# A hybrid sparse-attention and RWKV-7 block: the triangular inverse's levels split into two halves of the heads, and new delays in the order's table

## The chip, the cores and the metric

The kernel runs on 1 core of one Trainium2 chip. Times are device microseconds (us) of one execution. Before the change the median of 3 runs is 951.49 us (948.81 to 954.71).

## The reference, cut to what matters

One decoder block on x of 1 x 512 x 1024 in float32. After an RMS norm, one combined projection makes the columns of two branches that run side by side, and of two gates:

```
q, k = rms_norm(q), rms_norm(k)            # 8 heads of 64
scores = sum_h w_h * relu(q_idx_h . k_idx)  # the indexer, 8 heads of 64
sel = top_k(causal scores, 128)             # for each query
y_attn = softmax(q . k[sel] + rel_bias) @ v[sel]

for t in range(512):                        # RWKV-7, per head
    s_a = state @ (-kk_t)
    state = state * d_t + s_a b_t^T + v_t k_t^T
    y_t = state @ r_t
y_rwkv = (group_norm(y) + bonus * v) * g    # bonus = sum(r * k * r_k)

h = x + (sigmoid(g1) * (y_attn @ w_a) + sigmoid(g2) * (y_rwkv @ w_r)) @ w_out
out = h + (silu(n @ w_gate) * (n @ w_up)) @ w_down    # n = rms_norm(h), width 2816
```

## The kernel before, in words

**Weights and dense products.** All weights come in one stream of 129 chunks of 128x1024 floats. SP fetches a chunk, ACT rounds it to a high part, `w_hi` (L239), and POOL or, for every third chunk from number 17 on, DVE subtracts that from the raw chunk to make the low part, `w_lo` (L243). A dense product is three passes on PE for each 128 rows of the contraction: high by high, high by low, low by high (`dense_t`, L255 to L264), each a matmul of 512 columns. The activations' two parts are named `xnh` and `xnl`.

**The attention.** `queries` and `keys` (L471 to L515) take two heads at a time: ACT squares the projection from PSUM (L475, L493) and copies it; some time later `rest` sums the squares over a head on PE (`head_sums`, the "key sums"), POOL takes the power -0.5 (L500), ACT broadcasts it (L501), and, 6.5 units later, PE flips it, DVE multiplies, and ACT and DVE copy the parts of the keys (`split_heads`, L456 to L463, tiles `kh`, `kl`). DVE meanwhile runs the selection of the 128 keys, with rounds of MAX8 and MATCH_REPLACE. `attention` (L519) goes through 32 units, 4 blocks of 128 queries by 8 heads: one step makes the logits of a unit (tile `lg`, whose exponential is ACT's, L574), the flips of the unit two before (L169), and the product with the values `vt` of the one three before.

**The recurrence.** It is computed in 4 blocks of 128 tokens, each two chunks of 64. `operands` (L692) makes the scaled keys of a pair of heads, and its `rest` the bonus products from POOL's `ag` (L709). `matrices` (L740) makes the chunks' triangular matrices (`kr`, `kb`), and `invert` (L777 to L836) their inverses by doubling: five levels, in each of which PE multiplies `l16` (printed as `l` or `l_144`) by `tt` for 8 heads of 64 columns, DVE masks that into `rr` (L806), PE multiplies again twice, ACT copies one product to `tt` (L811) and DVE the other to `uu` (L814). All of these are f16 matmuls in PSUM tiles of tag "i", of which there are two banks. With 4 blocks that makes 20 levels. `steps` (L845) carries the state; `head_norm` (L917) normalises a block's output and multiplies by the gate of `zg` (`g2a`, `g2b`) on PE, in whose course POOL broadcasts the bonus to `bv` (L947) and DVE writes `zv`. The product `yr` (L1045 to L1049) needs the last head norm; it follows the second group of gates (`gr`, "gate matmuls").

**The order.** `Streams` (L98 to L122) writes the program's order before anything runs. Each part is a generator with a rank; it yields a delay, or the name of a signal to wait for. A clock, `st.now`, moves forward by a model time with each matmul, and of the parts whose time has come the one of lowest rank goes on. The dense products have rank 9, so they fill what the others leave. The delays stand in the table `L` (L89 to L91): `sums` before the key and query sums, `attn` between two steps of the attention for each block of queries, `bonus` before a bonus product, `inv_*` in the inverse. PE's instructions keep this order; on ACT, DVE and POOL the order follows from it.

Of the kernel before, what the change touches and what calls it, by code (L numbers as in the profile page):

```python
# [13 lines left out]
AF = mybir.ActivationFunctionType  # L14
# [4 lines left out]
H, N = 8, 64  # L19
# [63 lines left out]
for _n, _c in _PARS:  # L83
# [2 lines left out]

L = dict(norm=3.0, normed=1.3, score=0.4, pick=0.15, rms=6.5, sums=2.5, attn=(1.0, 0.6, 0.4, 0.35), attn_out=2.0, sig=0.3,  # L89
         prep=5.0, oper=6.0, bonus=6.0, mat=0.5, mats=2.8, inv_u=3.25, inv_t=1.4, inv_r=1.4, inv_n=0.9, inv_e=1.8,  # L90
         inv=1.8, vals=0.6, st_b=1.0, st_u=1.36, st_m=1.4, hn_b=4.55, hn_n=6.55, hn_g=2.0)  # L91
POOL_ONLY = 17
COPIES = 23
# [34 lines left out]
def hybrid_block(ctx: ExitStack, tc: tile.TileContext, x, first, rows, consts, lora, rel_bias, stream, out):  # L128
    nc = tc.nc
# [125 lines left out]
    def dense_t(ps, wt, c, act, t0=0, t1=S):  # L255

        k = len(act)
        for j in range(k):
            xh, xl = act[j][0][:, t0:t1], act[j][1][:, t0:t1]
            hi, lo = wt[j][0][:, c], wt[j][1][:, c]  # L260
            mm(ps, hi, xh, start=(j == 0), stop=False)
            mm(ps, hi, xl, start=False, stop=False)
            mm(ps, lo, xh, start=False, stop=(j == k - 1))
            yield 0.0  # L264

# [206 lines left out]
    def queries(j, ps):  # L472
# [15 lines left out]

        st.add(3, rest(), L["sums"])

# [285 lines left out]
    def invert(t):  # L776

        l16 = l16s[t % 2]
        U, T = blocks("uu", 1), blocks("tt", 1)
        nc.vector.tensor_mul(U, l16, lev1[:, None, :].to_broadcast([128, H, 128]))  # L780
        yield L["inv_u"]
        for g in range(2):
            ps = bank("i").rearrange("q (h t) -> q h t", h=4)
            for j in range(4):
                mm(ps[:, j], U[:, 4 * g + j], eye16, start=True, stop=True)
            nc.scalar.activation(T[:, 4 * g:4 * g + 4], ps, AF.Copy)
        for e in range(2):
            br = BLK[e]
            for g in range(2):
                hs = slice(g, H, 2)  # L790
                nc.gpsimd.tensor_sub(l16b[br, hs, br], A[t, e][g][br, :, br], l16[br, hs, br])
        yield L["inv_t"]
        for i in range(1, 6):
            s = 2 ** i
            two = lambda q, w: q.rearrange("q h (g w s) -> q h g w s", w=2, s=s)[:, :, :, w]
            one = lambda q, h, w: q[:, h].rearrange("q (g w s) -> q g w s", w=2, s=s)[:, :, w]
            four = lambda q: q.rearrange("q (h g s) -> q h g s", h=H, s=s)
            o = CONST_AT["level"][0] + (i - 1) * 64
            mask = con[:, o:o + 64].rearrange("q (g s) -> q g s", s=s)[:, None].to_broadcast([128, H, 64 // s, s])
            R = blocks("rr", 2)  # L800
            nc.gpsimd.tensor_copy(two(R, 1), eye16.rearrange("q (g w s) -> q g w s", w=2, s=s)[:, None, :, 1]  # L801
                                  .to_broadcast([128, H, 64 // s, s]))
            ps = bank("i")
            for h in range(H):
                mm(ps[:, h * 64:h * 64 + 64], l16[:, h], one(T, h, 0), start=True, stop=True)
            nc.vector.tensor_mul(two(R, 0), four(ps), mask)  # L806
            yield L["inv_r"]
            p1, p2 = bank("i"), bank("i")
            for h in range(H):
                mm(p1[:, h * 64:h * 64 + 64], U[:, h], one(R, h, 0), start=True, stop=True)  # L810
            nc.scalar.activation(two(T, 0), four(p1), AF.Copy)  # L811
            for h in range(H):
                mm(p2[:, h * 64:h * 64 + 64], R[:, h], one(U, h, 1), start=True, stop=True)
            nc.vector.tensor_copy(two(U, 1), four(p2))  # L814
            yield L["inv_n"]
        E = blocks("ee", 2, "rr")
        for g in range(2):
            ps = bank("i").rearrange("q (h t) -> q h t", h=4)
            for j in range(4):
                h = 4 * g + j  # L820
                mm(ps[:, j], l16b[:, h], T[:, h], start=True, stop=False)
                mm(ps[:, j], l16[:, h], T[:, h], start=False, stop=True)
            nc.vector.scalar_tensor_tensor(E[:, 4 * g:4 * g + 4], ps, -1024.0,
                                           eye1k[:, None, :].to_broadcast([128, 4, 128]), op0=OP.mult, op1=OP.add)
        yield L["inv_e"]
        U32 = unit("u32")
        for g in range(2):
            ps = bank("i").rearrange("q (h t) -> q h t", h=4)
            for j in range(4):
                mm(ps[:, j], E[:, 4 * g + j], U[:, 4 * g + j], start=True, stop=True)  # L830
            for q in BLK:
                hs = slice(4 * g, 4 * g + 4)
                nc.vector.scalar_tensor_tensor(hv(U32)[q, hs], ps[q, :, q], 1.0 / 1024.0, U[q, hs, q],
                                               op0=OP.mult, op1=OP.add)
        U32s[t] = U32
        st.signal(f"inv{t}", L["inv"])  # L836
# [374 lines left out]
```

## Time and profile before

| what | value |
|---|---|
| median of 3 runs | 951.49 us (948.81 to 954.71) |
| the profiled execution's own time | 951.66 us |
| its span in the trace | 949.9 us |
| PE busy (matmuls) | 911.4 us, 96% |
| DVE, ACT, POOL busy | 406.5, 344.5, 365.4 us |
| mean granted clock of PE | 0.99 |

The span runs from the first to the last instruction of the trace. Engines work side by side, so their busy times overlap; PE is TensorE's matmuls, DVE VectorE, ACT ScalarE, POOL GpSimd, SP the engine that issues most transfers. The stages by time, as the tiles in the trace show them: up to 50 us the norm and the first projections, to 107 us queries and keys with the selection, to 225 us the attention beside the projections of the recurrence, to 300 us the preparation of the recurrence, to 500 us its inverses and steps beside the gates, to 600 us the branch products and the output projection, and to the end the FFN.

### The profile page before, as it was taken

The page shows a single profiled execution, that of the slowest core. Times are in us where ns is not written, and L with a number is a line of the kernel's source. Part 1 is how long each engine was busy: PE and PEld are TensorE (multiplying, and loading weights), DVE is VectorE, ACT ScalarE, POOL GpSimd, SP SyncE. Part 2 cuts the span into 40 slices and gives each one's busy share as a digit, 9 for nine tenths or more (in the row PEclk, how much of TensorE's full clock was granted, in tenths as well). Part 3 has the DMA queues.
Part 4 walks back from the last instruction along what each step waited for, and adds up shares of the span by engine and source line. Part 5 has one row for each costly group of instructions (what it writes and reads, how often), then busy time and mean ns, then how long its engine had stood idle before and what let it go on. Part 6 is the DMA issues. An engine that isn't in the chain of part 4 may idle for free.

```text
span 949.9 us, 13573 instructions
## 1 busy us (share of the span) xinstructions
PE 911.4 (96%) x5526; PEld 765.4 (81%) x5526; DVE 406.5 (43%) x796; ACT 344.5 (36%) x548; POOL 365.4 (38%) x242
## 2 busy tenths in 40 slices
PE   7999899899989999999998999999999999999998
PEld 5988797688767777878886998888888888888886
DVE  4389898873573546573534616111111111100111
ACT  5554565543542433233423324323223232221120
POOL 6425532203264353525415632443534344432321
PEclk9999899999999999999999999999999999999999
DMA  6321232101222120201142332233232332332431
GB/s 230 92 79 44 88 117 68 45 1 59 86 67 67 46 67 23 68 20 50 46 133 79 94 94 68 89 94 106 88 111 89 99 101 90 91 108 89 138 107 44
DMA packets 24173, 77.77 MB, mean 82 GB/s; under 512 B 2869, under 2 KB 4366, under 8 KB 24112
## 3 DMA queue, kind: packets, MB, share of 16 engines
q1 hardware_dynamic: 20688, 72.49, 24.3%
q10 hardware_dynamic: 3424, 4.43, 1.7%
q8 instruction: 43, 0.70, 0.3%
q14 instruction: 18, 0.15, 0.0%
HBM read 74.53 MB, written 2.38 MB: 81 GB/s over the span
## 4 chain that ended last, share of the span: by engine, by line
PE 79%; DVE 11%; ACT 3%; POOL 3%; issue 3%; DMA 1%; SPq 0%; ACTq 0%; POOLq 0%; DVEq 0%
PE ps_d L162 57%; PE ps_c L162 11%; PE ps_i L162 9%; DVE score L437 2%; DVE max L436 2%; PE ps_c L169 2%; DVE score L424 1%; POOL w_lo L243 1%; DMA xa<-in_x_dram 1%; DVE qs L460 1%; PE ps_i L169 1%; ACT w_hi L239 1%; ACT lg L574 0%; POOL bb L700 0%; DVE w_lo L243 0%
## 5 line engine op out<-in xcount | busy, mean ns | idle before, releaser
L243 POOL TENSOR_TENSOR w_lo<-w_raw,w_hi 128x1024 fp32r<-128x1024 f32 (+1 forms) x94 | 221.1, 2354 | 366.8 <-ACT w_hi L239 360.0
L239 ACT ACTIVATE w_hi<-w_raw 128x1024 fp32r<-128x1024 f32 x129 | 136.6, 1060 | 370.9 <-PE ps_d L162 213.1
L162 PE MATMUL ps_d<-xnh,w_hi 128*128 128x512 f32 (+2 forms) x360 | 149.7, 416 | 0.0
L162 PE MATMUL ps_d<-hnl,w_hi 128*128 128x512 f32 (+1 forms) x368 | 139.9, 380 | 0.4 <-DVE hnl L336 0.4
L162 PE MATMUL ps_d<-hnh,w_hi 128*128 128x512 f32 (+1 forms) x368 | 139.9, 380 | 0.0
L162 PE MATMUL ps_d<-hnh,w_lo 128*128 128x512 f32 (+1 forms) x368 | 139.7, 380 | 0.0
L162 PE MATMUL ps_d<-xnh,w_lo 128*128 128x512 f32 (+2 forms) x360 | 137.6, 382 | 0.0
L162 PE MATMUL ps_d<-xnl,w_hi 128*128 128x512 f32 (+2 forms) x360 | 137.4, 382 | 0.0
L243 DVE TENSOR_TENSOR w_lo<-w_raw,w_hi 128x1024 fp32r<-128x1024 f32 x37 | 45.6, 1233 | 130.8 <-ACT w_hi L239 130.0
L1095 DVE TENSOR_TENSOR gsig<-ps_d,gsig 128x512 f32<-128x512 f32 x22 | 15.2, 692 | 157.6 <-PE ps_d L162 156.9
L162 PEld LDWEIGHTS ps_d<-hnl,w_hi 128*128 128x128 f32 x368 | 69.2, 188 | 13.8 <-DVE hnl L336 0.6
L162 PEld LDWEIGHTS ps_d<-hnh,w_lo 128*128 128x128 f32 x368 | 69.2, 188 | 13.1
L162 PEld LDWEIGHTS ps_d<-hnh,w_hi 128*128 128x128 f32 x368 | 69.2, 188 | 13.0
L162 PEld LDWEIGHTS ps_d<-xnh,w_lo 128*128 128x128 f32 x360 | 68.9, 191 | 13.1
L162 PEld LDWEIGHTS ps_d<-xnh,w_hi 128*128 128x128 f32 x360 | 69.4, 193 | 11.7 <-issue 2.6
L162 PEld LDWEIGHTS ps_d<-xnl,w_hi 128*128 128x128 f32 x360 | 69.4, 193 | 9.9 <-issue 1.9
L1099 POOL TENSOR_TENSOR ul<-gsig,uh 128x512 fp32r<-128x512 f32 x22 | 31.6, 1434 | 25.3 <-ACT uh L1098 25.3
L801 POOL COPY rr<-eye 128x512 f16<-128x512 f16 x20 | 13.5, 680 | 57.2 <-PE ps_i L162 57.2
L162 PE MATMUL ps_d<-w_hi,mh 128*128 128x256 f32 x120 | 34.0, 284 | 0.0
L162 PE MATMUL ps_d<-w_hi,ml 128*128 128x256 f32 x120 | 34.0, 283 | 0.0
L162 PE MATMUL ps_d<-w_lo,mh 128*128 128x256 f32 x120 | 34.0, 283 | 0.0
L574 ACT ACTIVATE lg<-lg,mx,qrs 128x128 f32<-128x128 f32 (+3 forms) x32 | 20.8, 649 | 22.1 <-DVE mx L573 22.0
(291 smaller groups left out, 1698.5 us busy)
## 6 DMA issues: line engine op xcount, KB each, us to landing
w_raw<-in_stream_dram SPq DMA_DIRECT2D x129, 512.0 KB, 3.6
xa<-in_x_dram SPq DMA_DIRECT2D x4, 512.0 KB, 5.8
ht<-in_x_dram ACTq DMA_DIRECT2D x8, 256.0 KB, 3.1
out_dram<-ht SPq DMA_DIRECT2D x8, 256.0 KB, 2.2
toep<-bias_table ACTq DMA_DIRECT2D x8, 128.0 KB, 3.4
gain<-in_rows_dram ACTq DMA_DIRECT2D x2, 256.0 KB, 3.1
con<-in_consts_dram SPq DMA_DIRECT2D x1, 321.0 KB, 6.9
bias_table<-tab ACTq DMA_DIRECT2D x1, 276.0 KB
```

The lines of the kernel that those rows point to most:

```text
L162: nc.tensor.matmul(o, w, r, **kw)
L169: nc.tensor.transpose(o, src, idn)
L239: nc.scalar.activation(hi, raw, AF.Copy)
L243: eng.tensor_sub(lo[:, o:o + n_], raw[:, o:o + n_], hi[:, o:o + n_])
L424: nc.vector.scalar_tensor_tensor(sc, r, w, sc, op0=OP.mult, op1=OP.add)
L436: nc.vector.max(m8, sc)
L437: nc.vector.match_replace(sc, m8, sc, TAKEN)
L460: nc.vector.scalar_tensor_tensor(lo[b, h], src[a], gain[a], hi[a, h], op0=OP.mult, op1=OP.subtract)
L574: nc.scalar.activation(lg, lg, AF.Exp, scale=scale, bias=mx[:, 2:3], accum_out=den[:, h:h + 1])
L801: nc.gpsimd.tensor_copy(two(R, 1), eye16.rearrange("q (g w s) -> q g w s", w=2, s=s)[:, None, :, 1] .to_broadcast([128, H, 64 // s, s]))
L1095: nc.vector.tensor_mul(g, pu, g)
L1099: nc.gpsimd.tensor_sub(ul, g, uh)
```

## The change

Four things. Three delays of the table are new: `sums` is 4.0 for 2.5, the four of `attn` are about equal, and `bonus` is 9.0 for 6.0. `dense_t` yields behind each of its three matmuls instead of behind every third, so that another part can come in between. And a level of the inverse works in two halves of four heads: the first product of heads 0 to 3, then, one delay `inv_h` on, that of heads 4 to 7, into the same PSUM tile; then, half by half, both second products into one tile, of which ACT copies the left 256 columns and DVE the right ones. `inv_r` and `inv_n` are shorter.

```diff
-L = dict(..., sums=2.5, attn=(1.0, 0.6, 0.4, 0.35), attn_out=2.0, sig=0.3,
-         prep=5.0, oper=6.0, bonus=6.0, mat=0.5, mats=2.8, inv_u=3.25, inv_t=1.4, inv_r=1.4, inv_n=0.9, inv_e=1.8,
+L = dict(..., sums=4.0, attn=(0.9, 0.9, 0.95, 1.0), attn_out=2.0, sig=0.3,
+         prep=5.0, oper=6.0, bonus=9.0, mat=0.5, mats=2.8, inv_u=3.25, inv_t=1.4, inv_h=0.25, inv_r=0.6, inv_n=0.5, inv_e=1.8,
...
             mm(ps, hi, xh, start=(j == 0), stop=False)
+            yield 0.0
             mm(ps, hi, xl, start=False, stop=False)
+            yield 0.0
             mm(ps, lo, xh, start=False, stop=(j == k - 1))
             yield 0.0
...
+            halves = slice(0, 4), slice(4, 8)
             ps = bank("i")
-            for h in range(H):
-                mm(ps[:, h * 64:h * 64 + 64], l16[:, h], one(T, h, 0), start=True, stop=True)
-            nc.vector.tensor_mul(two(R, 0), four(ps), mask)
-            yield L["inv_r"]
-            p1, p2 = bank("i"), bank("i")
-            for h in range(H):
-                mm(p1[:, h * 64:h * 64 + 64], U[:, h], one(R, h, 0), start=True, stop=True)
-            nc.scalar.activation(two(T, 0), four(p1), AF.Copy)
-            for h in range(H):
-                mm(p2[:, h * 64:h * 64 + 64], R[:, h], one(U, h, 1), start=True, stop=True)
-            nc.vector.tensor_copy(two(U, 1), four(p2))
-            yield L["inv_n"]
+            for hs in halves:
+                for h in range(hs.start, hs.stop):
+                    mm(ps[:, h * 64:h * 64 + 64], l16[:, h], one(T, h, 0), start=True, stop=True)
+                nc.vector.tensor_mul(two(R, 0)[:, hs], four(ps)[:, hs], mask[:, hs])
+                yield L["inv_h"] if hs.start == 0 else L["inv_r"]
+            for hs in halves:
+                pq = bank("i")
+                for h in range(hs.start, hs.stop):
+                    o = (h % 4) * 64
+                    mm(pq[:, o:o + 64], U[:, h], one(R, h, 0), start=True, stop=True)
+                for h in range(hs.start, hs.stop):
+                    o = 256 + (h % 4) * 64
+                    mm(pq[:, o:o + 64], R[:, h], one(U, h, 1), start=True, stop=True)
+                h4 = lambda q: q.rearrange("q (h g s) -> q h g s", h=4, s=s)
+                nc.scalar.activation(two(T, 0)[:, hs], h4(pq[:, 0:256]), AF.Copy)
+                nc.vector.tensor_copy(two(U, 1)[:, hs], h4(pq[:, 256:512]))
+                yield L["inv_h"] if hs.start == 0 else L["inv_n"]
```

What stands in the rows of three places, before and now (in the changed kernel, lines after L263 have numbers higher by 2, those behind the inverse by 9 more).

On ACT, at the second and third pair of keys: `ksq<-ps_d` is the Square, `kraw` the copy, `ksq<-qrs` the broadcast of POOL's power, `kh` the copies of the keys' high parts. Before:

```order
L493 ACTIVATE ksq<-ps_d 128x512
L494 ACTIVATE kraw<-ps_d,fst 128x512
L501 ACTIVATE ksq<-qrs 128x512 x2
L456 ACTIVATE kh<-kraw 64x512
L462 ACTIVATE kh<-kraw 64x512
L456 ACTIVATE kh<-kraw 64x512
L462 ACTIVATE kh<-kraw 64x512
L493 ACTIVATE ksq<-ps_d 128x512
L494 ACTIVATE kraw<-ps_d,fst 128x512
```

and now:

```order
L495 ACTIVATE ksq<-ps_d 128x512
L496 ACTIVATE kraw<-ps_d,fst 128x512
L503 ACTIVATE ksq<-qrs 128x512
L495 ACTIVATE ksq<-ps_d 128x512
L496 ACTIVATE kraw<-ps_d,fst 128x512
L503 ACTIVATE ksq<-qrs 128x512
L458 ACTIVATE kh<-kraw 64x512
L464 ACTIVATE kh<-kraw 64x512
```

The third pair's Square and copy have moved ahead of the second broadcast and of the four `kh` copies.

On PE, at the first product of a level of the inverse, with the semaphores that an instruction waits for: `ps_i<-tt,l_144` is the level's first product (8 matmuls, four to a half), `LDWEIGHTS` its weight load, `ps_d` a dense matmul. Before:

```order
L162 MATMUL ps_d<-xnh,w_lo 128x512
L162 LDWEIGHTS l_144
L162 MATMUL ps_i<-tt,l_144 128x64 [waits Activation_49]
L162 LDWEIGHTS l_144
L162 MATMUL ps_i<-tt,l_144 128x64
...
L162 MATMUL ps_d<-xnh,w_hi 128x512
```

and now, from the end of the first half on:

```order
L162 LDWEIGHTS l_144
L162 MATMUL ps_i<-tt,l_144 128x64
L162 MATMUL ps_d<-xnl,w_hi 128x512
L162 MATMUL ps_d<-xnh,w_lo 128x512
L162 LDWEIGHTS l_144 [waits DVE_49]
L162 MATMUL ps_i<-tt,l_144 128x64 [waits Activation_49]
L162 LDWEIGHTS l_144
L162 MATMUL ps_i<-tt,l_144 128x64
```

Two dense matmuls have come between heads 3 and 4, and the weight load of head 4 has a wait for DVE that stood nowhere inside the product before.

On PE, at the end of the last head norm: `ytok` is its flip, `zg` and `z_g_128` the products with the gate, `yr` the branch product behind it. Before:

```order
L162 MATMUL ps_d<-xnh,w_lo 128x512
L169 MATMUL ps_d<-fst,ytok 128x128 x4
L162 MATMUL ps_d<-zg,g2a 128x128
L162 MATMUL ps_d<-z_g_128,g2b 128x128
...
L162 MATMUL ps_d<-yr,w_hi 128x512 x2
```

and now:

```order
L169 MATMUL ps_d<-fst,ytok 128x128 x4
L162 MATMUL ps_d<-xnh,w_lo 128x512
...
L162 MATMUL ps_d<-zg,g2a 128x128
L162 MATMUL ps_d<-z_g_128,g2b 128x128
...
L162 MATMUL ps_d<-xnh,w_hi 128x512
L162 MATMUL ps_d<-xnl,w_hi 128x512
L162 MATMUL ps_d<-xnh,w_lo 128x512
...
L162 MATMUL ps_d<-yr,w_hi 128x512 x2
```

Ten dense matmuls stand now between the flips and the gate's products, and 75 between these and the first of `yr`; before there was none at either place.

## Rows read from the trace of the kernel before

**Rows 1.** Busy time by stage: stretch, length, PE, PEld, DVE, ACT, POOL, clock, DMA.

```profile
50.00:103.00 53.00, 51.88 (x252) 43.52 (x251) 49.73 (x115) 25.18 (x41) 22.81 (x9) 0.97 0.21 69
103.00:118.00 15.00, 10.71 (x60) 9.78 (x60) 11.30 (x27) 12.81 (x20) 6.49 (x4) 0.77 0.20 55
118.00:153.00 35.00, 33.18 (x238) 30.30 (x238) 34.27 (x89) 20.19 (x40) 11.73 (x6) 1.00 0.37 114
153.00:225.00 72.00, 65.48 (x424) 55.94 (x423) 52.45 (x173) 37.11 (x86) 12.32 (x10) 0.98 0.11 34
225.00:300.00 75.00, 70.00 (x319) 55.15 (x319) 40.38 (x64) 31.77 (x46) 35.36 (x25) 1.00 0.23 71
300.00:500.00 200.00, 196.17 (x1822) 159.31 (x1821) 106.28 (x171) 67.45 (x115) 76.95 (x75) 1.00 0.18 57
500.00:516.00 16.00, 12.20 (x57) 9.60 (x56) 6.57 (x10) 5.23 (x11) 6.94 (x5) 0.89 0.26 90
601.00:641.00 40.00, 40.00 (x179) 33.10 (x178) 4.53 (x5) 11.01 (x14) 17.82 (x10) 1.00 0.31 94
```

**Rows 2.** PE's waits: line, releaser, us in total, times, longest us.

```profile
PE ps_c L169 <- ACT lg L574: 7.7, 10, 1.7
PE ps_i L162 <- POOL ag L709: 5.0, 3, 2.8
...
PE ps_i L162 <- ACT ksq L493: 4.3, 1, 4.3
PE ps_d L162 <- ACT yr L1048: 3.5, 1, 3.5
...
PE ps_i L162 <- ACT tt L811: 1.8, 2, 0.9
PE ps_i L162 <- DVE uu L814: 1.6, 2, 0.8
```

**Rows 3.** Timeline, 103 to 109 us: start, us, instruction, idle before and releaser.

```profile
103.58 0.63 ACT L501 ACTIVATE ksq<-qrs 128x512 f32<-128x512 f32 x1 [5.56 <-POOL qrs L500]
...
106.71 0.57 ACT L493 ACTIVATE ksq<-ps_d 128x512 f32<-128x512 f32 x1
107.33 1.86 PE L162 MATMUL ps_i<-con,ksq 128*128 128x2 f32 x8 [4.29 <-ACT ksq L493]
```

**Rows 4.** Timeline of POOL ahead of a bonus product.

```profile
276.43 2.37 POOL L243 TENSOR_TENSOR w_lo<-w_raw,w_hi 128x1024 fp32r<-128x1024 f32 x1 [1.25 <-ACT w_hi L239]
278.76 1.70 POOL L709 TENSOR_TENSOR ag<-zr,ag 128x512 f32<-128x512 f32 x1
```

**Rows 5.** The chain that ended last, 500 to 516 us: start, us, what.

```profile
504.96 2.35 POOL w_lo L243
507.31 1.23 POOL bv L947
```

**Rows 6.** Timeline of a hand-off inside a level, and of a bank's wait.

```profile
384.23 0.41 PE L162 MATMUL ps_i<-tt,l 128*128 128x64 f16 x8
384.47 0.70 PE L162 MATMUL ps_d<-qs,w_hi 128*128 128x512 f32 x2
384.68 0.69 DVE L806 TENSOR_TENSOR rr<-ps_i,con 128x512 f16<-128x512 f32 x1 [0.24 <-PE ps_i L162]
385.01 0.40 PE L162 MATMUL ps_d<-qs,w_lo 128*128 128x512 f32 x1
...
371.87 0.69 DVE L814 CAST uu<-ps_i 128x512 f16<-128x512 f32 x1
372.62 1.16 PE L162 MATMUL ps_i<-kr,kb 64*128 64x128 f32 x8 [0.78 <-DVE uu L814]
```

**Rows 7.** Groups by line and shape: busy us, mean ns, idle before and releaser.

```profile
L243 DVE TENSOR_TENSOR w_lo<-w_raw,w_hi 128x1024 fp32r<-128x1024 f32 x37 | 45.6, 1233 | 130.8 <-ACT w_hi L239 130.0 <-issue 0.2
L1075 DVE TENSOR_TENSOR ht<-ps_d,ht 128x256 f32<-128x256 f32 x15 | 5.8, 420 | 19.0 <-PE ps_d L162 19.0
L1012 ACT ACTIVATE vt<-ps_d 128x256 f32<-128x256 f32 x8 | 2.6, 372 | 2.3 <-PE ps_d L162 2.2
```

More of the change, by code (lines that the diff above doesn't have):

```diff
@@ L85 @@
     NPAR += _c
-L = dict(norm=3.0, normed=1.3, score=0.4, pick=0.15, rms=6.5, sums=2.5, attn=(1.0, 0.6, 0.4, 0.35), attn_out=2.0, sig=0.3,
-         prep=5.0, oper=6.0, bonus=6.0, mat=0.5, mats=2.8, inv_u=3.25, inv_t=1.4, inv_r=1.4, inv_n=0.9, inv_e=1.8,
+L = dict(norm=3.0, normed=1.3, score=0.4, pick=0.15, rms=6.5, sums=4.0, attn=(0.9, 0.9, 0.95, 1.0), attn_out=2.0, sig=0.3,
+         prep=5.0, oper=6.0, bonus=9.0, mat=0.5, mats=2.8, inv_u=3.25, inv_t=1.4, inv_h=0.25, inv_r=0.6, inv_n=0.5, inv_e=1.8,
          inv=1.8, vals=0.6, st_b=1.0, st_u=1.36, st_m=1.4, hn_b=4.55, hn_n=6.55, hn_g=2.0)
```

## The prediction

> **What bounds the kernel now.** I read the busy time by stage first. PE (TensorE) is busy for 40.00 us of the 40 us in the FFN, where 179 matmuls of 512 columns take 0.2235 us each, and for 196.17 of 200 us between 300 and 500 us; so PE bounds the kernel, and its work is the same after the change (as many matmuls of each shape). Only PE's idle time, the time at the half clock and the cost of going from one kind of matmul to another can change. They lie in five stretches [rows 1]: 103 to 118 us (10.71 of 15 us busy, granted clock 0.77), 153 to 225 us (65.48 of 72), 225 to 300 us (70.00 of 75), 300 to 500 us, and 500 to 516 us (12.20 of 16, clock 0.89). Next comes the list of what PE waits for: the attention's flips for the exponentials on ACT, 7.7 us in 10 waits; the bonus products for POOL, 5.0 in 3; the key sums for ACT, 4.3 in one; the yr product for ACT, 3.5 in one; and the bank of the inverse's matmuls, some 3.4 us in four waits [rows 2]. The reader is to see that no wait inside a level of the inverse is in that list: its hand-offs are covered by dense matmuls now.
>
> **The change part by part.** All sums are made against the profiled execution, 951.66 us (span 949.9 us), which is 0.17 us above the median of the three runs.
>
> *Later sums.* At 107.33 us PE waits 4.29 us for the Square of the third key pair. That ACTIVATE ran at 106.71 us although its input was there, since ACT, which works in order, had stood 5.56 us for POOL's power of the pair before, and then did the copies to kh [rows 3]. In the new order of ACT it stands ahead of that second broadcast and of the kh copies, and the sums come some 6 dense matmuls (1.3 us) later. So this wait goes, and with it the half clock behind it: 0.77 over 15 us is 6.9 us at 1.2 GHz, the lower of its two levels (15 x 0.23 x 2), of which about 4.4 fall on work, 2.2 us lost. The whole would be 6.5 us. But DVE is what PE meets next. It is busy 49.73 of 53 us before and 34.27 of 35 us after this place with the selection; in both orders 43 of the 48 MATCH_REPLACE stand ahead of the first attention operation on DVE. The attention's first flip can come earlier only by what DVE idles here, 15 minus 11.30 or 3.7 us [rows 1]; PE, back 6.5 us earlier, waits for the rest there. I take 2 us off (bounds: 6.5 us off, and 1 us on if the wait that takes its place brings the clock down again).
>
> *Even attention delays.* From the second block of queries a step has 5 dense matmuls between its parts instead of 3, 0.45 us more; a flip comes two steps after its logits, so the exponential has 0.9 us more. Of the ten waits the longest was 1.7 us and the mean 0.8. The dense work for this is there: before, 102 dense matmuls lay between the end of the attention and the preparation, and now 64. PE's idle time in 153 to 225 us is 6.5 us, and the clock of 0.98 costs 72 x 0.04 / 2 = 1.4 us. Of these 7.9 us I take 6 off (2 to 8). DVE is at 73% there and is not in the way [rows 1].
>
> *Later bonus products.* A product waits for POOL's ag, 5.0 us in three waits, at most 2.8 [rows 2]; POOL did a w_lo of 2.37 us first, which had itself waited for ACT [rows 4]. The products now stand behind at least 12 more dense matmuls (2.7 us), for all but the last pair. I take 4 us off (2 to 5). If POOL were the bound the wait would only move, but it is busy 35.36 of 75 us here.
>
> *The end of the recurrence.* Before, the dense gates are used up when the last head norm comes: PE stands while POOL's w_lo (2.35 us) and bv, then DVE's zv, run [rows 5], 3.8 us in 500 to 516 us, and the clock of 0.89 costs 16 x 0.22 / 2 = 1.8 us. The inverse's levels now hold about 10 dense matmuls each instead of 15, so the recurrence ends earlier and 75 gate matmuls (16.8 us) are left behind the last head norm. Its whole chain fits under them: 5.5 us off (5 to 7).
>
> *The inverse in halves: switches.* After a block of f16 matmuls, the first two dense ones take 385.01 - 384.47 = 0.54 us, and two in the steady flow 0.45 (twice 0.2235): a switch costs 0.09 us [rows 1, 6]. The order has 78 such switches for 36 before, and 6 fewer behind the matrices' products: 36 x 0.09 = 3.3 us on (2 to 4.5). Nothing hides this; PE itself is slower.
>
> *The inverse in halves: the bank.* Both halves of the first product write one PSUM bank. In the new order the load of the weights of the second half waits for DVE, which there reads the first half: a wait that the old order hasn't. Worked out: the last of eight f16 matmuls ends 0.41 us after the first starts, and DVE starts 0.04 us behind that; four, issued in half of the 0.24 us that eight take, end after 0.29. A product of half the size on DVE is nearest to the 0.420 us of a 128x256 from PSUM (0.690 for 512 columns) [rows 6, 7]. DVE's end to PE's start is 372.62 less 372.56 or 0.06 us. So the second half can start 0.29 + 0.04 + 0.42 + 0.06 = 0.81 us after the first. PE is there after 0.12 us of matmuls and two dense ones with their switch, 0.54: 0.66 us. It stands 0.15 us in 17 of the 20 levels (three have more work between), if DVE is free at once. DVE is busy 106.28 of 200 us [rows 1], mostly with operations of 0.42 to 0.69 us, so half of the time it comes some 0.3 us late: 0.15 more. 17 to 18 levels x 0.3 = 5.5 us on. The bounds are 0 (a load that PE takes early, other work between) and 20 x 1.23 = 25 us, if DVE's w_lo of 1.233 us stood in front each time [rows 7]. I take the value nearest to the usual DVE operation.
>
> *The inverse in halves: the next level.* T and U of a half lie in one bank too, and in the new order DVE's copy of U waits for ACT's copy of T. Both take 0.41 + 0.04 + 0.37 + 0.05 + 0.42 + 0.06 = 1.35 us from the half's first matmul, where PE comes back to that bank after its own matmuls, two dense ones, the other half's and three dense ones, 0.24 + 0.54 + 0.24 + 0.77 = 1.79 us. The slack of 0.44 us is used up only where ACT or DVE is busy: 20 x 0.1 = 2 us on (0 to 5). The matrices' products, which waited 3.4 us for a bank (0.78 us for the copy of U in the row shown [rows 6]), come behind shorter copies but in tighter places: 1 us off (3 off to 1 on). DVE and ACT get 60 more instructions, which cost nothing beyond this while the dense matmuls cover them. The turns behind each matmul cost nothing by themselves.
>
> The Trainium skill, "PSUM — Partial Sum Buffer", section "PSUM bank collisions raise a hardware error", says that two engines may not be in one bank and quadrant at once, even in different columns, and that PSUM is to be guarded by bank, not by address. This rule speaks against halves that share a bank, and the new order keeps it; no run here shows a collision. Without the wait that it asks for, the sum below would be 5.5 us lower.
>
> Sum: 2 + 6 + 4 + 5.5 = 17.5 us off; 3.3 + 5.5 + 2 - 1 = 9.8 us on; 951.66 - 7.7 = 944.0 us.
>
> **The rivals.** *The levels' waits are covered.* The steps of the recurrence fall between halves, and PE stays ahead. For it: no hand-off inside a level waits now. Against it: 17 of the 20 first halves have two dense matmuls and nothing else behind them. Only the switches are left: 951.66 - 17.5 + 3.3 - 1 = 936.5 us.
>
> *The waits only move to the selection.* DVE at 98% in 118 to 153 us holds the attention; the sums give nothing and the clock falls again (1 us on), the flips of the first two blocks still wait (3 off instead of 6), the rest as above: 951.66 + 1 - 3 - 4 - 5.5 + 9.8 = 950 us. For it speaks DVE's busy time; against it, that PE idles only 1.8 of 35 us where DVE is that full, and 6.5 of 72 us behind it, where DVE is at 73% [rows 1].
>
> *DVE late at each first half: slower.* The place is the weight load of the second half, 20 times. The price is what DVE has in hand: if the product of the first half stands each time behind an operation like w_lo (1.233 us), the term of 5.5 becomes 25, and the time 944 + 19.5 = 963.5 us. It decides against the change from 7.7 / 20 = 0.4 us of further lateness per level on. For it: w_lo and the 0.69 us operations of matrices and head norms fall into the same levels; against it: DVE idles nearly half of that stage.
>
> *The halves are only reordered, with no effect on the end.* If the gates left over at the end were needed in the attention, the end's 5.5 us would stay: 949.5 us. The order speaks against it with its 75 matmuls.
>
> **How the numbers follow.** A measurement can tell about 1% from no change: 942.0 and 961.0 us are the bounds. The forecast, 944 (939 to 948), gets 0.50, of which a quarter lies under 942; the covered levels, 936.5, 0.28; the waits that move (and the end that stays), 950, 0.14; late DVE, 963.5, 0.08, nearly all of it over 961. Faster by over 1%: 0.125 + 0.28 and a little of the rest, 0.42; slower 0.07; within 1% 0.51. The range takes in the covered levels with a little more from the sums, and part of late DVE: 932 to 955 us; the likeliest case's own is 939 to 948.
>
> **What would show it.** Right: no wait of the key sums for ACT and none of yr; granted clock 1.00 near 512 us; flips waiting under 3 us in all; PE's weight loads waiting for the halves of rr on DVE some 0.3 us each, 5 to 6 us in all; first dense matmuls behind f16 ones still 0.09 us longer. Wrong: no such wait on rr (then 936.5), waits on rr over 0.7 us each (then over 951), or a long wait for DVE at the first flip with the clock at half behind it.

## The result, and the profile after

The changed kernel takes 941.12 us (median of 4 runs, 940.72 to 944.05); the kernel before, run beside it, 951.88 us (4 runs, 948.81 to 954.71). The ratio is 0.9894, with a 95% interval of 0.9857 to 0.9931: 10.8 us faster, where 7.7 were forecast. The profiled execution took 941.39 us, its span is 939.6 us.

First the busy time by stage, after. The columns are those of [rows 1]; the last stages begin earlier here, since the recurrence ends earlier.

```profile
103.00:118.00 15.00, 15.00 (x114) 14.24 (x113) 14.64 (x35) 11.82 (x18) 6.75 (x4) 1.00 0.38 109
118.00:153.00 35.00, 30.11 (x198) 26.28 (x197) 32.68 (x78) 21.44 (x46) 11.17 (x5) 0.95 0.29 92
153.00:225.00 72.00, 68.60 (x447) 59.81 (x447) 53.24 (x172) 36.73 (x82) 14.91 (x10) 1.00 0.14 41
225.00:300.00 75.00, 74.98 (x355) 57.98 (x354) 49.91 (x73) 33.48 (x50) 39.38 (x32) 1.00 0.23 71
300.00:490.00 190.00, 184.56 (x1743) 144.70 (x1742) 106.25 (x207) 68.52 (x132) 71.26 (x70) 1.00 0.18 54
490.00:510.00 20.00, 20.00 (x90) 16.55 (x89) 5.85 (x8) 6.48 (x9) 7.74 (x4) 1.00 0.33 104
595.00:635.00 40.00, 40.00 (x178) 33.12 (x177) 6.44 (x7) 11.06 (x14) 17.03 (x9) 1.00 0.32 96
```

Against [rows 1], PE's hole at 103 to 118 us is closed (15.00 of 15 us for 10.71), and part of it has come back in 118 to 153 us (4.9 us idle for 1.8, clock 0.95 for 1.00). The attention's later part, 153 to 225 us, idles 3.4 us for 6.5; the preparation of the recurrence nothing for 5.0; the stretch around the first `yr` nothing for 3.8. Only the inverse's stage is worse: 5.4 us idle in 190 where there were 3.8 in 200. The FFN is as it was.

PE's waits after, to be read against [rows 2]:

```profile
PE ps_c L169 <- ACT lg L576: 6.1, 6, 2.2
...
PE ps_i L162 <- DVE rr L811: 2.6, 5, 0.7
PE ps_i L169 <- ACT ksq L503: 2.0, 1, 2.0
...
PE ps_i L162 <- DVE uu L823: 1.6, 4, 0.5
```

The waits for `ag` and for `yr` are gone. That of the key sums for the Square is gone too; what is left of the keys' chain is one wait of 2.0 us of the flip behind it. The flips wait in 6 places for 10, but the longest is now 2.2 us. New is the wait for `rr`, in five places.

The new wait at close range: a level with DVE free, and one with DVE busy, in the timeline (start, us, engine, instruction, idle before and releaser).

```profile
314.03 0.29 PE L162 MATMUL ps_i<-tt,l 128*128 128x64 f16 x4
...
314.36 0.42 DVE L811 TENSOR_TENSOR rr<-ps_i,con 128x256 f16<-128x256 f32 x1
314.47 0.40 PE L162 MATMUL ps_d<-xnh,w_hi 128*128 128x512 f32 x1
314.83 0.17 PEld L162 LDWEIGHTS <-l 128*128 128x128 f16 x4 [0.41 <-DVE rr L811]
314.84 0.29 PE L162 MATMUL ps_i<-tt,l 128*128 128x64 f16 x4
```

```profile
402.85 0.29 PE L162 MATMUL ps_i<-tt,l 128*128 128x64 f16 x4
...
402.99 0.68 DVE L980 SCALAR_TENSOR_TENSOR mrg<-mrg,ps_d 128x512 f32<-128x512 f32 x1
...
403.58 0.42 DVE L823 CAST uu<-ps_i 128x256 f16<-128x256 f32 x1
403.91 0.42 DVE L811 TENSOR_TENSOR rr<-ps_i,con 128x256 f16<-128x256 f32 x1
404.38 0.17 PEld L162 LDWEIGHTS <-l 128*128 128x128 f16 x4 [1.13 <-DVE rr L811]
```

In the first the second half's matmuls start 314.84 - 314.03 = 0.81 us after the first half's, the number that the prediction worked out. In the second DVE has two operations in hand, and it is 1.53 us to the weight load. Of the 20 pairs in the trace, nine stand 0.80 to 0.81 us apart, four 0.86 to 0.88 and six 1.18 to 1.54, one of these with eight other matmuls between; in the last pair 36 come between. The list above counts the late ones alone: in the usual case the dense matmul ahead is busy until 314.87 us in the profile, so the wait shows as no idle time of PE.

### The profile page after: what moved, and what is told of

It is laid out like the page before. It is cut to its first block, busy times and chain, and to the rows that moved or that the text cites. A ratio compares the mean times of both kernels' runs of the same rounds, so it can differ in the third digit from the quotient of the medians.

```text
span 939.6 us, 13659 instructions
## 1 busy us (share of the span) xinstructions
PE 910.5 (97%) x5526; PEld 759.4 (81%) x5526; DVE 417.1 (44%) x836; ACT 347.4 (37%) x568; POOL 364.3 (39%) x242
## 3 DMA queue, kind: packets, MB, share of 16 engines
q1 hardware_dynamic: 20688, 72.49, 24.6%
## 4 chain that ended last, share of the span: by engine, by line
PE 83%; DVE 10%; ACT 3%; issue 2%; POOL 1%; DMA 1%; SPq 0%; ACTq 0%; POOLq 0%; DVEq 0%
PE ps_d L162 60%; PE ps_c L162 11%; PE ps_i L162 9%; DVE score L439 2%; PE ps_c L169 2%; DVE max L438 2%; POOL w_lo L243 1%; DMA xa<-in_x_dram 1%; DVE kl L459 1%; ACT w_hi L239 1%; DVE lg L569 0%; DVE xs L330 0%; DVE w_lo L243 0%; ACT lg L576 0%; PE ps_i L169 0%
## 5 line engine op out<-in xcount | busy, mean ns | idle before, releaser
L162 PE MATMUL ps_d<-xnh,w_hi 128*128 128x512 f32 (+2 forms) x360 | 142.0, 395 | 0.0
L162 PE MATMUL ps_d<-xnl,w_hi 128*128 128x512 f32 (+2 forms) x360 | 141.7, 394 | 0.0
L162 PE MATMUL ps_d<-xnh,w_lo 128*128 128x512 f32 (+2 forms) x360 | 141.6, 393 | 0.0
L243 DVE TENSOR_TENSOR w_lo<-w_raw,w_hi 128x1024 fp32r<-128x1024 f32 x37 | 47.5, 1283 | 129.8 <-ACT w_hi L239 129.3
```

The lines of the kernel that those rows point to most:

```text
L162: nc.tensor.matmul(o, w, r, **kw)
L243: eng.tensor_sub(lo[:, o:o + n_], raw[:, o:o + n_], hi[:, o:o + n_])
```

## The experiments

Three terms of the sum were in doubt: what the halves cost (the bank, the switches), whether the end's gain is theirs, and what the later sums bring while DVE is full. Each kernel's time stands beside runs of the kernel before on the same chip. The runs beside 954.84 us were taken on another chip than those beside 951.78 and 952.78; across the two the ratios are to be compared, not the times. "Turns" are the two `yield 0.0` in `dense_t`, "full width" is the level of before with all eight heads at once, and a "switch" is a change from f16 matmuls of the inverse to a dense one.

| kernel | us, median | before, us | ratio (95% interval) |
|---|---|---|---|
| changed | 941.12 | 951.88 | 0.9894 (0.9857 to 0.9931) |
| changed, again | 941.44 | 951.78 | 0.9866 (0.9826 to 0.9906) |
| full-width inverse, all else new | 936.73 | 952.78 | 0.9826 (0.9771 to 0.9881) |
| the same, shorter delays | 939.18 | 952.78 | 0.9839 (0.9781 to 0.9897) |
| the same, longer inv_r | 938.13 | 951.78 | 0.9824 (0.9771 to 0.9877) |
| only halves | 959.44 | 952.78 | 1.0068 (1.0036 to 1.0100) |
| only turns | 945.53 | 951.78 | 0.9932 (0.9904 to 0.9960) |
| only the three delays | 940.46 | 951.78 | 0.9855 (0.9813 to 0.9897) |
| only the sums | 954.07 | 954.84 | 0.9999 (0.9973 to 1.0025) |
| changed, two banks | 937.59 | 952.78 | 0.9829 (0.9781 to 0.9878) |
| changed, longer inv_h | 945.02 | 954.84 | 0.9911 (0.9879 to 0.9943) |
| full width, wider attention | 930.82 | 954.84 | 0.9762 (0.9728 to 0.9796) |
| two banks, wider attention | 933.76 | 954.84 | 0.9791 (0.9762 to 0.9820) |

**The halves undone.** The changed kernel with the full-width level and its old delays:

```diff
-            halves = slice(0, 4), slice(4, 8)
...
+            ps = bank("i")
+            for h in range(H):
+                mm(ps[:, h * 64:h * 64 + 64], l16[:, h], one(T, h, 0), start=True, stop=True)
...
-inv_h=0.25, inv_r=0.6, inv_n=0.5
+inv_r=1.4, inv_n=0.9
```

> The changed kernel with the inverse's levels at full width again, with their old delays; the turns and the three other delays stay. Theory A (the halves only cost: 0.81 us from the first half's start to the second's where two dense matmuls fill 0.66, 35 more switches at 0.09 us, and the turns alone leave the gates at the end): some 3.2 us of switches, 5.1 us of waits for the bank and 1.6 us of later hand-offs go, 2.7 us of bank waits at the kr,kb matrices come back: 934 us (931 to 937), no wait of yr. Theory B (as the prediction put it: the halves shorten the recurrence and so the end's 5.5 us hang on them): 939.5 us, with the yr wait back. Rival C (the halves are what gains): over 944 us.

Measured: 936.73 us, between the theories' 934 and 939.5, and no wait for `yr` in the trace: the halves cost time, and the end's gain doesn't need them. By the medians they cost 4.4 us; the two executions of this kernel at a granted clock of 0.998 took 934.94 and 935.03 us, 6.1 under the changed kernel, which had 0.995. What lies above 934 us in the slower two goes with the clock: the profiled one (940.73 us) has it at half for 10 us in the inverse's stage (below).

**The halves alone.** The kernel before with the new level and `inv_h=0.25, inv_r=0.6, inv_n=0.5` for `inv_r=1.4, inv_n=0.9`.

> The kernel before with only the inverse in halves and its three delays; no turns, and the old delays elsewhere. Its order keeps no gate matmul behind the last head norm and puts three dense matmuls where the changed kernel has two. Theory A (halves cost, the end comes from the turns): the waits of the key sums, the flips, the bonus products and yr stay, 41 more switches at 0.09 us cost 3.7 us, three dense matmuls with a switch (0.76 us) and 0.12 us of PE's own cover the 0.81 us where DVE is free at once: 952 + 3.7 + 1 to 3 for a late DVE, some 1 to 2 off at the matrices: 955 us (952 to 960). Theory B (the halves end the recurrence earlier): 949 us, no yr wait.

Measured: 959.44 us, 6.7 over before. From its list of PE's waits (line, releaser, us in total, times, longest):

```profile
PE ps_i L162 <- POOL ag L709: 5.0, 3, 2.8
...
PE ps_i L162 <- ACT ksq L493: 4.3, 1, 4.3
PE ps_d L162 <- ACT yr L1054: 3.8, 1, 3.8
PE ps_i L162 <- DVE rr L808: 2.0, 4, 0.6
```

The `yr` wait is there, in full. Theory B falls. Part of what lies above 955 us is the clock again, in the stage of the bonus products, whose order is that of before:

```profile
228.00:310.00 82.00, 76.99 (x328) 60.58 (x326) 40.11 (x64) 33.06 (x47) 37.48 (x26) 0.94 0.21 65
```

At 0.94 the 82 us lose at most 82 x 0.06 = 4.9 us in the profiled execution (965.39 us, the slowest of ten from 954.97 on), where [rows 1] have 1.00.

**The turns alone.** The kernel before with

```diff
             mm(ps, hi, xh, start=(j == 0), stop=False)
+            yield 0.0
             mm(ps, hi, xl, start=False, stop=False)
+            yield 0.0
```

> The kernel before with only the turn behind each of the three matmuls of a dense product. The same delays are now met after fewer dense matmuls: 12 in a level of the inverse for 15, 5 and 2 between two attention steps for 6 and 3, and 60 gate matmuls are left behind the last head norm, where the order of before has none. Theory A (the turns bring the end's gain): no yr wait and no half clock near 510 us, 5.8 us off; the flips wait longer (16 units of the last blocks, up to 0.3 us each, 2 to 5 us on), key sums and bonus products wait as before: 950 us (946 to 953), PE waiting some 10 us for lg. Theory B (the end hangs on the halves): the yr wait of 3.5 us stays, 955 us.

Measured: 945.53 us, 6.2 off. Its waits:

```profile
PE ps_c L169 <- ACT lg L576: 9.4, 11, 1.9
...
PE ps_i L162 <- POOL ag L711: 2.8, 4, 1.6
...
PE ps_i L162 <- ACT ksq L495: 1.9, 2, 1.3
```

No wait for `yr`: the end's gain is the turns'. Without them a delay of 1.4 is met at the next third matmul, 9 dense ones later, with them after 7, so a level with nothing else in it sinks from 15 dense matmuls to 12. Counted in the traces from the first level to the last, 248 dense matmuls remain of 306, 18 fewer stand ahead of the first level, and 60 lie behind the last head norm. The halves alone have 12 in such a level, too, but still in threes: 291 in all, and the 15 saved are used up ahead of the last head norm's flips (96 there for 81). The flips wait longer, as expected (9.4 us for 7.7); key sums and bonus products wait 4.6 us less, which was not expected and is about what is missing from 950.

**The three delays alone**, `sums=4.0`, `attn=(0.9, 0.9, 0.95, 1.0)` and `bonus=9.0` in the kernel before.

> The kernel before with only the three new delays for the sums, the attention and the bonus products; no turns, no halves. Theory A: in the changed kernel's trace these stages lost 12.0 us less (sums 3.8, attention 3.2, bonus 5.1); here the attention has six dense matmuls between most steps for five, so its waits go further down; yr still waits 3.5 us: 940 us (937 to 943). Rival (the stages' gain needs the finer turns): flips still wait over 6 us, 946 us.

Measured: 940.46 us, 11.3 off, as expected and as much as the whole change:

```profile
PE ps_d L162 <- ACT yr L1048: 3.5, 1, 3.5
PE ps_c L169 <- ACT lg L574: 3.3, 7, 1.9
...
PE ps_i L162 <- POOL ag L709: 1.2, 1, 1.2
```

With six dense matmuls between most attention steps `lg` waits 3.3 us, where the changed kernel with five has 6.1. So the turns take back some of what the delays give, one dense matmul in each step. No run has the attention's delays or the bonus's alone; how the 11.3 us divide is read from traces.

**The sums alone**, `sums=4.0` in the kernel before.

> The kernel before with only the later sums (4.0 for 2.5). As the prediction put it (DVE's selection is what PE meets next): the wait of 4.3 us and the half clock at 105 us go, the first flip of the attention waits longer: 950 us (948 to 951.5), 2 us off. Rival (the selection isn't in the way): 945.5 us, all 6.5 us off. Other rival: the wait only moves whole, 952 us.

Measured: 954.07 us against 954.84, ratio 0.9999: nothing that can be told from zero. Its busy time by stage:

```profile
90.00:135.00 45.00, 43.85 (x308) 40.56 (x307) 43.58 (x94) 30.95 (x50) 23.20 (x11) 1.00 0.33 99
135.00:225.00 90.00, 81.23 (x490) 68.53 (x489) 66.83 (x218) 43.82 (x101) 17.14 (x12) 0.94 0.14 43
225.00:308.00 83.00, 78.06 (x323) 60.93 (x321) 39.67 (x64) 32.60 (x46) 37.78 (x26) 0.92 0.21 64
```

The wait of 4.3 us and the half clock behind it are gone, and the first flip waits 1.92 us for 1.37. But the clock stands at 0.94 and 0.92 in the two stages behind, where [rows 1] have 0.98 in 153 to 225 us and 1.00 in 225 to 300. What is lost to the clock is at most the stretch times what the clock lacks of 1.00: 90 x 0.06 = 5.4 and 83 x 0.08 = 6.6 us, the latter in a stage whose order is that of before, with about the same waits for `ag` (4.9 us for 5.0). So in the profiled execution (956.76 us; the ten runs go from 948.73 to 957.11) what the sums gain is lost again there; that the sums are the cause isn't shown, since the kernel before has executions of up to 957.33 us beside them. From 50 to 230 us PE is busy 167.93 us for 166.25 in the kernel before, 1.7 us less idle, near the 2 us of the prediction. The interval is 2.5 us wide on either side, so the times can tell such a gain neither from nothing nor from the rival in which the wait only moves; the gain of 6.5 us is ruled out.

**A bank for each half.** In the changed kernel:

```diff
-            ps = bank("i")
             for hs in halves:
+                ps = bank("i")
```

> The changed kernel with each half of the first product in a PSUM bank of its own (the two banks of the tag taken in turn, as for the second products), so that PE's second half needn't wait for DVE to have read the first. Theory A (the bank costs PE 0.15 us in each of 17 levels and 0.5 to 0.9 in five, 5.1 us in all): 936 us (934 to 938), no wait on rr ahead of a second half. Rival (the hand-off is late anyway, the wait moves to the second products): 941 us.

Measured: 937.59 us, 3.5 us below the changed kernel's 941.12 (3.9 below its second measurement). The level that was shown above:

```profile
313.29 0.29 PE L162 MATMUL ps_i<-tt,l 128*128 128x64 f16 x4
...
313.61 0.42 DVE L811 TENSOR_TENSOR rr<-ps_i,con 128x256 f16<-128x256 f32 x1
313.73 0.40 PE L162 MATMUL ps_d<-xnh,w_hi 128*128 128x512 f32 x1
313.96 0.17 PEld L162 LDWEIGHTS <-l 128*128 128x128 f16 x4 [0.27 <-issue]
313.96 0.29 PE L162 MATMUL ps_i<-tt,l 128*128 128x64 f16 x4
```

The second half follows after 0.67 us, with no wait for DVE: the wait was the bank's. In 13 of the 20 pairs it now follows after 0.67 to 0.69 us; six stay at 0.81 to 1.48, three of these with other matmuls between. Added up, the second halves come 3.85 us earlier than in the changed kernel, as much as the times tell. So some 3.5 us is what the bank costs, for 5.5 in the sum.

**A longer inv_h**, `inv_h=0.6` for 0.25 in the changed kernel.

> The changed kernel with inv_h 0.6 for 0.25: three dense matmuls between the halves for two, 25 gate matmuls left behind the last head norm. Three dense with a switch (0.76 us) and PE's own 0.12 cover the 0.81 us that the second half needs where DVE is free at once. Theory A: some 13 waits of 0.14 to 0.20 us go, the five late ones shrink by 0.22 each: 3.4 us off, 938 us (937 to 940), PE waiting for rr under 2 us, no yr wait. Rival (what the halves cost is switches alone): 941.4 us, within 1 us.

Measured: 945.02 us, a miss by 7 us on the wrong side. Beside the kernel before on its chip this is a ratio of 0.9911, for 0.9894 and 0.9866 of the changed kernel; the intervals overlap, so that it is slower than the changed kernel isn't shown, only that the 3.4 us didn't come. Where DVE is free the second half now comes 0.90 us behind the first and waits for nothing, as worked out; but the waits for `rr` add up to 3.9 us in 4 places, and one of them is 2.46 us:

```profile
446.07 2.36 POOL L243 TENSOR_TENSOR w_lo<-w_raw,w_hi 128x1024 fp32r<-128x1024 f32 x1
...
446.65 2.33 DVE L936 TENSOR_TENSOR ytok<-ytok,yrs 128x512 f32<-128x512 f32 x1
...
448.90 0.41 DVE L811 TENSOR_TENSOR rr<-ps_i,con 128x256 f16<-128x256 f32 x1
...
449.37 0.29 PE L162 MATMUL ps_i<-tt,l 128*128 128x64 f16 x4 [2.46 <-DVE rr L811]
```

Each level is longer, other parts fall to other places in it, and here the head norm's product on DVE stands ahead of `rr` (why it takes 2.33 us is told in the last section). More cover for the usual case, which costs 0.14 us, doesn't help against such a late one. It isn't all: PE's other waits in the inverse grow and shrink with the new places, and 2.4 us of new waits lie in the keys' chain and at a `w_lo`, ahead of the inverse, as in the other profiles from that chip that have the new delays.

**Shorter and longer full-width levels.** The full-width kernel with `inv_r=1.06, inv_n=0.6`, then with `inv_r=1.6`; and the changed kernel once more as reference.

> As the run before, but with inv_r 1.06 for 1.4 and inv_n 0.6 for 0.9: about 8 dense matmuls in a level of 15 before, 122 gate matmuls left behind the last head norm. Worked out from the full-width hand-off, 0.41 + 0.04 + 0.69 + 0.06 = 1.20 us from the level's first matmul, of which 0.24 are PE's own: five dense matmuls with their switch, 1.2 us, cover it. Theory A: 934 us (931 to 938), within 2 us of the run before, PE waiting little for rr and somewhat more for tt or uu (under 4 us in all). Rival: DVE is often late, each of 20 levels waits 0.3 us or more: 940 us.

> The full-width inverse with turns and the three delays, but inv_r 1.6 for 1.4: 13 dense matmuls in a level, 42 gate matmuls left behind the last head norm. In the full-width run with 12 the profile shows the half clock for 10 us near 392 to 409 us, in that with 8 for 20 us near 345 us, in the kernel before with 15 nowhere in that stage. If fewer dense matmuls between the small f16 ones are what brings the clock down: full clock in 300 to 500 us, 933 us (931 to 936), no yr wait. If the clock falls by chance from execution to execution: like the run with 12, 936 us (934 to 940).

> The changed kernel once more, on the same chip as the three others, as their reference: 941 us (940 to 944), and a second profile of it, to see whether the clock falls at the same places (64 and 143 us).

Measured: 939.18, 938.13 and 941.44 us; the first is above its range, the second within that of the clock falling by chance, and in the second profile of the changed kernel the clock falls at the same two places as in the first. In the kernel with 8 dense matmuls PE waits little more than in that with 12 (29.0 us idle in all for 28.4, and a single wait for `rr`), so the rival that had each level wait falls; what it loses is the clock. At the same granted clock of 0.996 the two took 938.42 to 939.76 and 938.43 us. One line each of the busy time by window, of the full-width kernel with 12, with 8, and of the kernel with the turns alone:

```profile
385.00:412.00 27.00, 24.59 (x216) 19.96 (x214) 17.22 (x29) 8.11 (x14) 8.94 (x9) 0.81 0.01 2
```

```profile
340.00:370.00 30.00, 28.38 (x218) 23.64 (x219) 16.62 (x29) 8.57 (x15) 9.62 (x13) 0.66 0.01 2
```

```profile
300.00:460.00 160.00, 155.29 (x1570) 126.29 (x1570) 99.36 (x158) 55.40 (x98) 64.83 (x70) 1.00 0.14 45
```

Worked out as above, the first two lose up to 27 x 0.19 = 5.1 and 30 x 0.34 = 10.2 us against the full clock. That fewer dense matmuls bring the clock down falls: the kernel with 13 has 0.97 over its stage, and the kernel with the turns alone has the same order of PE in this stage as the one with 12, matmul for matmul, and there the clock is 1.00. It differs from execution to execution; what decides it wasn't found.

**The attention's delays wider.** The full-width kernel, and the kernel with two banks, both with `attn=(1.1, 1.1, 1.1, 1.1)` for `(0.9, 0.9, 0.95, 1.0)`.

> The full-width inverse with turns and new delays (the run of 936.7 us), and the attention's four delays at 1.1: six dense matmuls between most steps for five, as the run with the delays alone had them, where PE waited 3.3 us for lg against 6.2 us with five. 60 gate matmuls still stand behind the last head norm. Theory (the flips' wait for the exponential is a matter of one more dense matmul, 0.22 us a step): lg waits near 3.5 us, 934 us (931 to 937), the spread of some 2 us left to the clock in the inverse's stage. Rival (the first flip waits for DVE's selection and the rest moves with it): 936.7 us, within 1 us.

> The halves with two banks for the first product (937.6 us), and the attention's delays at 1.1. The same 3 us off: 934.5 us (932 to 937). Its inverse had no half clock in the profile where the full-width one had 10 us of it; if that is of the form of the work, this one ends below the full-width run by 1 to 3 us; if it is chance, the two agree within 1 us, or the full-width one is lower for its 35 switches fewer (3.2 us).

Measured: 930.82 and 933.76 us, the fastest of all. In the first, `lg` is down to

```profile
PE ps_c L169 <- ACT lg L576: 1.7, 5, 0.7
```

and the clock is full in the inverse's stage of both. So these two compare the inverses cleanly: the halves with a bank each cost 2.9 us against full width, for 35 more switches (78 for 43), 0.084 us each. In the traces PE idles alike in the two (24.6 and 25.0 us) and is busy 3.8 us longer with the halves, 0.11 us a switch. The gain of the wider delays at full width, 5.9 us by the medians and 6.1 by the ratios, is over the 3 us expected of it: PE idles 3.4 us less, and the rest goes with the clock, which isn't at half between 127 us and the end. The four runs lie within 0.6 us, where the kernel before spreads over 7.6 us in the 13 beside them.

## Why the prediction was right, and where it wasn't

**The sum.** Off: 17.5 us forecast. The two profiled executions bear it out as a whole: from 50 to 225 us PE idles 3.6 us less and is 6.8 us less at the half clock, worth up to 3.4 (7.0 for the 8 of sums and attention), from 225 to 300 us 5.0 less (for 4), at the end some 5.5. On: 9.8 forecast; 2.9 for the switches and 3.5 for the bank make 6.4. So what was too high is the cost, by some 3 us, and the change came out at 10.8 us for 7.7. The runs of the parts agree, the delays' 11.3 + the turns' 6.2 - 6.4 = 11.1 us, though not in each piece: delays and turns together, at full width, gave 16.1 and not 17.5.

**Switches**, 3.3 us forecast: 2.9 for 35 by the times, 3.8 by PE's busy time. Right.

**The bank**, 5.5 us: 3.5. The mechanism was right to the hundredth (0.81 us where DVE is free). DVE was late in fewer places than assumed, five of 20 pairs and not half of them, but by more, 0.37 to 0.73 us for 0.3. What was too high is the share of it that the bank causes, since some of the second halves are late with a bank of their own, too. The bound of 25 us, DVE late each time, didn't come.

**Next level and matrices**, 2 - 1 = 1 us: about nothing is left for them when switches and bank are taken from what the halves cost. In the list of waits `tt` is gone, and `uu` has 1.6 us where the two had 3.4.

**Bonus**, 4 us: PE idles 0.02 us of 75 in 225 to 300 us for 5.0, and no wait for `ag` is left. Right, and a little better.

**Attention**, 6 us, and **sums**, 2 us: the sum came out (7.0), the picture did not. PE idles 3.1 us less in 153 to 225 us and 4.3 less in 103 to 118, but 3.1 more in 118 to 153. The flips still wait 6.1 us, where the prediction named under 3 as a sign of being right, and one of its signs of being wrong is there, a long wait at the first flip with the half clock behind it:

```profile
140.77 0.49 ACT L576 ACTIVATE lg<-lg,mx,qrs 128x128 f32<-128x128 f32 x1 [3.83 <-DVE mx L575]
141.41 0.33 PE L169 MATMUL ps_c<-fst,lg 128*128 128x128 f32 x1 [2.22 <-ACT lg L576]
...
145.05 0.63 PE L162 MATMUL ps_d<-xnh,w_hi 128*128 128x512 f32 x1
```

The exponential on ACT had itself waited for DVE's maximum `mx`, and DVE has MAX8 and MATCH_REPLACE of the selection in between. So that DVE is what PE meets next was right: the first flip comes 3.4 us earlier (141.41 for 144.82 us), under the 3.7 that the prediction gave as the most. Behind it a dense matmul takes 0.63 us where it takes 0.39 at the full clock. That the total fits is in part luck: 3.4 of the 7.0 us come from the half clock, which differs from execution to execution, and what the sums bring by themselves is less than the runs can tell.

**The end**, 5.5 us, is the step that failed in its reason: "The inverse's levels now hold about 10 dense matmuls each instead of 15, so the recurrence ends earlier" takes halves and turns as one, the fourth rival asks whether "The halves are only reordered, with no effect on the end", and of the turns it says only that they "cost nothing by themselves". The size was right: the 3.8 us of idle time and the clock of 0.89 are gone, the last gate product on DVE ends at 485.56 us (484.87 + 0.69), and `yr` starts at 501.63 us without a wait:

```profile
484.87 0.69 DVE L964 TENSOR_TENSOR zv<-bv,ps_d 128x512 f32<-128x512 f32 x1 [9.72 <-PE ps_d L162]
...
501.63 0.62 PE L162 MATMUL ps_d<-yr,w_hi 128*128 128x512 f32 x2
```

But it is the turns that bring it: 60 of the 75 gate matmuls are there without the halves, and these suffice. The halves without the turns leave no gate matmul for the end and lose 6.7 us; the halves could be left out and the kernel would be faster. The order of the kernel before with each of the two edits alone would have told that beforehand.

**The rivals.** The covered levels (936.5) fell: second halves wait. The waits that move (950) fell by the number; what is seen of them is the wait and the half clock at the first flip. Late DVE (963.5) is seen in five of 20 levels, not in all. That the halves do nothing for the end (949.5) was near the truth, but the turns did it.

## What to carry to other kernels

Take an edit of several parts apart: here the one named first costs time (4.4 us between the medians, 6.4 worked out from its parts), and the gain at the end comes from a side remark, two `yield`s. Where an order is made by delays, count the filler between two steps in the order itself, since the size of the filler's pieces rounds every delay up. Splitting a step into halves for overlap has to be cheaper than the wait that was there: in this kernel [rows 2] have no wait inside a full-width level, the shared bank cost 3.5 us, and even with a bank each the more frequent changes between kinds of matmul (0.08 to 0.11 us each) cost 2.9. A wait may cost more than its length, by the half clock that can follow it. Here the versions with the fewest waits had the least of it, and their runs lay closest together; that the one is the cause of the other isn't shown.

## What the runs showed of the hardware

An operation on DVE whose inputs both lie in SBUF is held up while POOL runs its subtraction. The product of the head norm, `ytok` by `yrs`, takes 0.68 us in three of its four places in the changed kernel and 0.94 in the fourth, none of them beside a `w_lo` of POOL, and 2.33 and 2.23 us in the two places of the kernel with the longer `inv_h` where it starts during one. The first of these ends at 448.98 us, 0.55 us after POOL's `w_lo` ends (446.07 + 2.36 = 448.43 us): it looks as if it began only then. The changed kernel has the same in other places, here at the keys, where a subtraction on DVE that takes 0.69 us with no `w_lo` of POOL beside it takes 1.94 and ends at 122.87 us, again 0.55 us after POOL's end at 122.32 us:

```profile
119.94 2.38 POOL L243 TENSOR_TENSOR w_lo<-w_raw,w_hi 128x1024 fp32r<-128x1024 f32 x1
120.93 1.94 DVE L459 TENSOR_TENSOR kl<-kraw,kh 64x512 fp32r<-64x512 f32 x1
```

The Trainium skill, "SBUF — State Buffer", section "SBUF: two separate sides", says that DVE with two SBUF inputs and a GpSimd operation that reads SBUF take one pair of ports in turn, the first holding it for its whole instruction. The trace agrees: in all three places the operation on DVE that started second ends after the other, with 0.55 us left to do in the two worked out above.

The half clock isn't a matter of the order alone. Two kernels with the same matmuls in the same order from the first `kr,kb` product to the end of the inverses, and with about the same waits there (4.6 and 4.7 us of PE idle), ran that stage at 0.97 and 1.00. In the three full-width executions in which it fell there, each fall began 1.5 to 2.7 us behind the end of a wait of PE of 0.78 to 1.13 us; the kernel with the turns alone has four waits of 0.79 to 1.06 us there, and no fall. So a wait came ahead of each of these falls, but not a fall behind each wait.
